# Expert-choice layers of a two-layer diffusion block: weight chunks in runs of 8 KB, token gathers spread over the experts, layer norms in pairs

## The chip, the cores and the metric

One core of one Trainium2 chip runs the whole program in one launch. The metric is device time in microseconds (us), the median of three runs. A lower time is better.

## The reference, cut to what matters

The block has two layers on 256 latent tokens and 256 context tokens of width 1024, all in float32. Each layer mixes tokens by four branches, projects, normalises, and then runs an expert-choice feed-forward part: each of 16 experts picks its 32 best tokens of a stream (latent or context), and its output goes back to those tokens, weighted by the gate.

```python
x = layer_norm(alpha * x + g1 * y, ln1_g, ln1_b)
h = x * (1 + sc2) + sh2
aff = softmax(h @ w_router)                     # 256 tokens x 16 experts
gval, idx = top_k(aff.T, 32)                    # 32 tokens of each expert
xg = h[idx]
y = (silu(xg @ w_gate) * (xg @ w_up)) @ w_down  # three 1024 x 1024 matrices per expert
f = zeros.at[idx].add(y * gval)
x = layer_norm(alpha * x + g2 * f, ln2_g, ln2_b)
```

In layer 0 this is done for both streams (context and latent have their own modulation but share the experts); in layer 1 for the latent stream alone. The expert weights are 2 x 16 x 3 matrices of 4 MB.

## The kernel before

Tokens lie on the 128 partitions, so a tile of tokens is 128 x 1024: tiles 0 and 1 are the context, 2 and 3 the latent stream. `xz` holds the tiles of the residual stream (four in layer 0, two in layer 1). The program text is a dataflow; a scheduler orders each engine's instructions when the program is built, by program order as priority and by readiness, so instructions of neighbouring steps are interleaved, and each engine then runs its list in order.

`out_project` (L1167) writes the last mixer result into `xz`. With the last column group (g = 3) it takes for each tile the statistics (`ln_stats`, L1207: two `bn_stats`, one `bn_aggr`, and `rsqrt`, L109, a chain of 11 small VectorE operations on 128 x 1), then for the tile before it the router logits (`route`, L1276: eight transposes, two copies, eight matmuls, two VectorE operations) and the normalisation in place (`ln_hat`, L1220). The last tile's normalisation stands in `moe` at L1369.

`moe` (L1297) issues the loads of expert 0's weights first, then softmax and top-k on VectorE (L1357 to L1391), then the experts. Weights come in chunks of 256 rows, 1 MB each: 12 chunks an expert, 192 a layer, all issued by SP in the order in which they are used (`wl`, L1326). A chunk's 256 rows are laid as `(k p) f -> p k f`: row p and row 128 + p on partition p, so each partition gets two runs of 4 KB. Slots are taken in turn from a list: buffers of 2048 floats per partition take a whole chunk in one DMA (tile `w`, or `we` where the tile has another name); pairs of 1024 floats take the two halves in two DMAs of 512 KB (`we`). Layer 0 has 13 slots in turn, 7 of them whole; layer 1 has 18, of which 11 are whole. A few chunks of expert 0 go to tiles that are free only then (`early`, L1320): in layer 0 three of the four `xg` tiles. A chunk's slot is free when its last matmul has read it; SP waits for that before it issues the next DMA in line, and everything behind it on SP waits as well.

`gather(g)` (L1398) builds the inputs of four experts, transposed, as `xgT`: one-hot matrices OH by VectorE (one operation per token tile and stream), then matmuls of 128 x 128 of `xz` with OH, each of them two PE records since float32 takes two passes: 64 records a group in layer 0, 32 in layer 1, with an ACT or DVE evacuation each. Group 0 is interleaved with expert 0's matmuls; group 1 comes in expert 1 after gate and up, group 2 in expert 2 after gate and up, group 3 at the end of expert 2, followed by `residual` (L1430), which overwrites `xz` by `alpha * (xz * g + b)` with 32 PE records and 8 to 16 VectorE operations. After every fourth expert the outputs `ys` are scattered into `xz` (L1505 to L1537). The last scatter is added in PSUM (`fin_tiles`, L1539), and `ln_last` (L1227) normalises one tile after the other: in layer 0 one half of a tile by ACT and one by DVE, and layer 1 begins with `make_h` (L267), which transposes the tiles; in layer 1 it writes the output.

Of the kernel before, what the change touches and what calls it, by code (L numbers as in the profile page):

```python
# [91 lines left out]
class Net:  # L92
# [1074 lines left out]
    def out_project(self, l):  # L1167
# [39 lines left out]
    def ln_stats(self, t, src=None):  # L1207

        nc = self.nc
        z = self.xt(t)  # L1210
        st = self.sm.tile([P, 2, 6], F32, tag="bst", name="bst")
        for j in range(2):
            nc.vector.bn_stats(st[:, j], src[j] if src else z[:, j * 512:(j + 1) * 512])
        mv = self.sm.tile([P, 2], F32, tag="bmv", name="bmv")
        nc.vector.bn_aggr(mv, st)
        rs = self.sm.tile([P, 1], F32, tag="brs", name="brs")
        self.rsqrt(rs, mv[:, 1:2], 1, "l")
        return mv[:, 0:1], rs

    def ln_hat(self, t, stats=None):  # L1220

        nc = self.nc
# [4 lines left out]
    def ln_last(self, l, t, src, rows):  # L1227

        nc = self.nc
        z = self.xt(t)  # L1230
        mu, rs = self.ln_stats(t, src)
        if l == 0:
            nb = self.sm.tile([P, 1], F32, tag="lnb", name="lnb")
            nc.vector.tensor_scalar(nb, mu, rs, -1.0, op0=OP.mult, op1=OP.mult)
            nc.scalar.activation(z[:, 0:512], src[0], AF.Identity, scale=rs, bias=nb)
            nc.vector.tensor_scalar(z[:, 512:1024], src[1], mu, rs, op0=OP.subtract, op1=OP.mult)
# [519 lines left out]
```

## Time and profile before

| what | value |
|---|---|
| median of three runs | 2164.75 us (2156.14 to 2170.97) |
| the profiled execution's own time | 2166.49 us |
| its span, first to last instruction | 2164.7 us |
| PE busy | 1849.5 us (85%) |
| DVE, ACT, POOL busy | 946.1, 503.9, 341.2 us |
| DMA moved | 553.92 MB, mean 256 GB/s |
| DMA share of queue q1 | 66.2% of 16 engines' span |

The whole program is one core's; busy times are sums over stages with different limits, so they are read by stage. The share of the DMA engines and GB/s over 40 slices of 54 us show two stretches at about 409 GB/s: the experts of layer 0 (about 720 to 1205 us) and of layer 1 (about 1695 to 2146 us). PE runs at a granted clock of 2.4 GHz where the row says 1.00 and at 1.2 GHz where it says 0.50.

### The profile page before, as it was taken

Reading aid. Unit: us, or ns where it says so; the run is one execution under the profiler, and the core shown is the slowest. Engines: PE = TensorE matmul, PEld = TensorE weight load, DVE = VectorE, ACT = ScalarE, POOL = GpSimd, SP = SyncE. Lnnn points to the kernel's source line nnn. Section 1 sums busy time; section 2 is a strip of 40 time slices with the busy share of each in tenths; the row PEclk is TensorE's granted clock in tenths of the full one; section 3 lists DMA queues with packets and bytes.
Section 4 is the critical chain, followed back from the end, with each engine's and each line's share of the span. In section 5 each row is a group of like instructions: output and inputs, shape, how many; then the busy total and the mean of one; then the engine's idle time right before and its main releaser. Section 6 shows DMA issues by size and latency. Waiting matters only on the chain. (4 is left out here: it accounts for less than half of the span.)

```text
span 2164.7 us, 33549 instructions
## 1 busy us (share of the span) xinstructions
PE 1849.5 (85%) x13730; PEld 1198.9 (55%) x13730; DVE 946.1 (44%) x2139; ACT 503.9 (23%) x1037; POOL 341.2 (16%) x366
## 2 busy tenths in 40 slices
PE   6899899988999899988887898898989886676665
PEld 2677778877879454322222576788889542222221
DVE  3859457854226324121121586967655330010102
ACT  2332217742221110000000332346443110000000
POOL 1151320014431000000000134321274000000000
PEclk9999999999999899999999998989999897776867
DMA  7546412137333599999999465303487899999996
GB/s 291 175 157 209 147 65 88 40 115 251 112 136 112 220 385 347 410 409 409 409 409 409 161 227 183 98 23 106 151 271 268 325 408 409 409 409 409 409 409 255
DMA packets 200182, 553.92 MB, mean 256 GB/s; under 512 B 16223, under 2 KB 83165, under 8 KB 194397
## 3 DMA queue, kind: packets, MB, share of 16 engines
q1 hardware_dynamic: 190960, 538.56, 66.2%
q10 hardware_dynamic: 9068, 13.23, 1.7%
q8 instruction: 108, 1.77, 0.3%
q14 instruction: 46, 0.37, 0.1%
HBM read 541.25 MB, written 10.49 MB: 255 GB/s over the span
## 5 line engine op out<-in xcount | busy, mean ns | idle before, releaser
L1461 PE MATMUL ps_gu<-w,xgT 128*32 128x256 f32 (+1 forms) x1632 | 241.5, 534 | 68.3 <-DMA w<-in_w_up_e_dram 35.0
L149 POOL TENSOR_TENSOR wl<-w,wh 128x1024 fp32r<-128x1024 f32 x62 | 155.2, 2503 | 894.6 <-ACT wh L148 805.4
L1461 PE MATMUL ps_gu<-we,xgT 128*32 128x256 f32 (+1 forms) x1440 | 204.0, 509 | 44.2 <-DMA we<-in_w_up_e_dram 26.3
L1461 PEld LDWEIGHTS ps_gu<-w,xgT 128*32 128x32 f32 (+1 forms) x1632 | 78.3, 134 | 210.5 <-issue 81.1
L1503 DVE TENSOR_TENSOR y<-ps_dn,g2r 32x512 f32<-32x512 f32 (+1 forms) x128 | 70.9, 554 | 254.3 <-PE ps_dn L1492 252.8
L311 PE MATMUL ps_gate<-hh,wh 128*128 128x512 f32 (+1 forms) x512 | 179.4, 351 | 0.4 <-ACT wh L148 0.4
L313 PE MATMUL ps_gate<-hh,wl 128*128 128x512 f32 (+1 forms) x512 | 179.7, 351 | 0.0
L312 PE MATMUL ps_gate<-hl,wh 128*128 128x512 f32 (+1 forms) x512 | 178.2, 348 | 0.0
L148 ACT CAST wh<-w 128x1024 fp32r<-128x1024 f32 x124 | 129.3, 1048 | 178.1 <-PE ps_gate L312 78.2
L1461 PEld LDWEIGHTS ps_gu<-we,xgT 128*32 128x32 f32 (+1 forms) x1440 | 62.0, 127 | 171.9 <-DMA we<-in_w_up_e_dram 63.7
L1492 PE MATMUL ps_dn<-w,eaT 128*32 128x256 f32 (+1 forms) x896 | 119.3, 524 | 28.8 <-DMA w<-in_w_down_e_dram 21.9
L1471 ACT ACTIVATE eth<-ps_gu 128x512 f32<-128x512 f32 (+1 forms) x32 | 15.7, 491 | 515.8 <-PE ps_gu L1461 515.8
L312 PE MATMUL ps_n<-wl,hh 128*128 128x256 f32 x400 | 116.6, 291 | 6.7 <-POOL wl L149 6.7
L1474 DVE SCALAR_TENSOR_TENSOR eac<-eth,ps_gu 128x512 f32<-128x512 f32 (+1 forms) x32 | 17.7, 555 | 238.9 <-PE ps_gu L1461 238.9
L311 PE MATMUL ps_n<-wh,hh 128*128 128x256 f32 x400 | 117.4, 294 | 5.5 <-DVE c_qk L872 3.6
L149 DVE TENSOR_TENSOR wl<-w,wh 128x1024 fp32r<-128x1024 f32 x62 | 85.8, 1384 | 72.4 <-ACT wh L148 72.1
L313 PE MATMUL ps_n<-wh,hl 128*128 128x256 f32 x400 | 116.7, 292 | 0.0
L1492 PE MATMUL ps_dn<-we,eaT 128*32 128x256 f32 (+1 forms) x640 | 91.2, 492 | 17.6 <-DMA we<-in_w_down_e_dram 13.2
L311 PEld LDWEIGHTS ps_gate<-hh,wh 128*128 128x128 f32 x512 | 98.9, 193 | 11.2 <-ACT wh L148 0.8
L313 PEld LDWEIGHTS ps_gate<-hh,wl 128*128 128x128 f32 x512 | 99.1, 193 | 10.8 <-DVE wl L149 0.2
L312 PEld LDWEIGHTS ps_gate<-hl,wh 128*128 128x128 f32 x512 | 98.7, 193 | 10.8
L1473 DVE SCALAR_TENSOR_TENSOR eth<-eth,ps_gu 128x512 f32<-128x512 f32 (+1 forms) x32 | 17.8, 555 | 193.6 <-ACT eth L1471 193.6
(452 smaller groups left out, 3579.4 us busy)
## 6 DMA issues: line engine op xcount, KB each, us to landing
w<-in_w_gate_e_dram SPq DMA_DIRECT2D x75, 1024.0 KB, 13.2
w<-in_w_down_e_dram SPq DMA_DIRECT2D x72, 1024.0 KB, 12.7
w<-in_w_up_e_dram SPq DMA_DIRECT2D x62, 1024.0 KB, 13.3
we<-in_w_up_e_dram SPq DMA_DIRECT2D x120, 512.0 KB, 13.6
w<-in_w_in_dram SPq DMA_DIRECT2D x54, 1024.0 KB, 5.6
we<-in_w_down_e_dram SPq DMA_DIRECT2D x108, 512.0 KB, 14.0
we<-in_w_gate_e_dram SPq DMA_DIRECT2D x96, 512.0 KB, 13.6
w<-in_w_mod_dram SPq DMA_DIRECT2D x44, 1024.0 KB, 5.1
```

The costliest lines, as they stand in the source:

```text
L148: nc.scalar.copy(h, w)
L149: (nc.gpsimd if j else nc.vector).tensor_tensor(x, w, h.bitcast(F32), op=OP.subtract)
L311: nc.tensor.matmul(ps, lh[k], rh[k], start=(k == 0), stop=False)
L312: nc.tensor.matmul(ps, lh[k], rl[k], start=False, stop=False)
L313: nc.tensor.matmul(ps, ll[k], rh[k], start=False, stop=(k == nk - 1))
L1461: nc.tensor.matmul(ps[M * q:M * q + M, :NF], xg[e // 4][:, 2 * kk + k, e % 4, :], w[k][:, q * NF:(q + 1) * NF], start=(kk == 0 and k == 0) ...
L1471: nc.scalar.activation(th, pss[0][:, :NF], AF.Tanh, scale=0.5)
L1473: nc.vector.scalar_tensor_tensor(th, th, 1.0, pss[0][:, :NF], op0=OP.add, op1=OP.mult)
L1474: nc.vector.scalar_tensor_tensor(ac, th, 0.5, pss[1][:, :NF], op0=OP.mult, op1=OP.mult)
L1492: nc.tensor.matmul(py[M * q:M * q + M, :NF], av[:, fc % nj, fc // nj, :], w[k][:, q * NF:(q + 1) * NF], start=(fc == 0), stop=(fc == 7))
L1503: nc.vector.tensor_tensor(ys[w][32 * e4:32 * e4 + 32, q * NF:(q + 1) * NF], py[o:o + 32, :NF], g2r[o:o + 32, q * NF:(q + 1) * NF], op=OP.mult)
```

## The change

1. Expert weights: a chunk's rows are laid as `(p k) f`, so that partition p gets rows 2p and 2p + 1, which lie next to each other in memory. A whole chunk becomes one run of 8 KB a partition; halves stay runs of 4 KB, now every second row. What the weights multiply is laid to match: features are taken in pairs (`pairs`), so the transposes of `xz`, of the activations and the gather's stationary operand read every second float. The modulation columns are brought into that order by `in_pairs` (16 small matmuls in layer 0, 8 in layer 1, two copies), the router's weights by their DMA.
2. `residual` writes to own tiles `acc` and `xz` stays, so that gathers can come later: group 1 in expert 2, group 2 in expert 6, group 3 in expert 10. `residual` moves to the end of expert 1. `xg` has two buffers in place of four; `acc` takes their room, and takes part of the early chunks.
3. Norms: two tiles share one `rsqrt` chain. In `out_project` the statistics are taken for pairs; the last two tiles are normalised by ACT in `moe`. `ln_last` runs for two tiles; in layer 0 ACT does three of four halves.
4. The one-hot operations of a group become one operation.

```diff
@@ merge
+        oh = self.mg.tile([P, 2, 512], F32R, tag="oh", name="oh", bufs=1)
         nc.sync.dma_start(oT[:, :, :n], self.oT[br])
         ol = self.mg.tile([P, 2, 512], F32R, tag="ol", name="ol", bufs=1)
-        oh = self.mg.tile([P, 2, 512], F32R, tag="oh", name="oh", bufs=1)
@@ out_project
                 if g == 3:
-                    stats[t] = self.ln_stats(t)
                     if t > t0:
-                        self.route(t - 1, stats[t - 1])
-                        self.ln_hat(t - 1, stats[t - 1])
-        self.route(3, stats[3])
-        self.last_stats = stats[3]
+                        pl[t - 1] = self.route(t - 1)
+                    if t % 2:
+                        mu, rs = self.ln_pair([self.halves(t - 1), self.halves(t)])
+                    elif t > t0:
+                        for i in range(2):
+                            self.logits(i, pl[i], mu[:, i:i + 1], rs[:, i:i + 1])
+                        for i in range(2):
+                            self.ln_hat(i, mu[:, i:i + 1], rs[:, i:i + 1])
+        pl[3] = self.route(3)
+        for i in range(2):
+            self.logits(2 + i, pl[2 + i], mu[:, i:i + 1], rs[:, i:i + 1])
+        self.last_stats = mu, rs
+    def pairs(x):
+        return x.rearrange("p (a q j) -> p a j q", q=P, j=2)
+    def ln_pair(self, srcs):
+        mv = self.sm.tile([P, 2, 2], F32, tag="bmv", name="bmv")
+        for i, src in enumerate(srcs):
...
+                nc.vector.bn_stats(st[:, j], src[j])
+            nc.vector.bn_aggr(mv[:, i], st)
+        self.rsqrt(rs, mv[:, :, 1], 2, "l")
+    def ln_hats(self, t, mu, rs):
+        nc.vector.scalar_tensor_tensor(nb, mu, -1.0, rs, op0=OP.mult, op1=OP.mult)
+        for i in range(2):
+            z = self.xt(t + i)
+            nc.scalar.activation(z, z, AF.Identity, scale=rs[:, i:i + 1], bias=nb[:, i:i + 1])
@@ ln_last (layer 0)
+                    if i and j:
+                        nc.vector.tensor_scalar(o, src[i][j], mu[:, i:i + 1], r, op0=OP.subtract, op1=OP.mult)
+                    else:
+                        nc.scalar.activation(o, src[i][j], AF.Identity, scale=r, bias=nb[:, i:i + 1])
+    def in_pairs(self, name, cols):
...
+        for i, c in enumerate(cols):
+            cv = c.rearrange("p (a h) -> p h a", h=2)
+            for h in range(2):
+                for j in range(2):
+                    nc.tensor.matmul(pv[64 * h:64 * h + 64, j, i], self.c("ident").rearrange("p (m j) -> p j m", j=2)[:, j],
+                                     cv[:, h], start=True, stop=True)
...
@@ route
-                nc.tensor.transpose(ps[j][:, k * P:(k + 1) * P], z[:, kc * P:(kc + 1) * P], self.c("ident"))
+                nc.tensor.transpose(ps[j][:, k * P:(k + 1) * P], self.pairs(z)[:, kc // 2, kc % 2], self.c("ident"))
@@ moe
-                early = {x: [(px, "xg", 4)] for x in (7, 8, 9)}
+                early = {7: [(px, "xg", 2)], 8: [(px, "acc", 2)], 9: [(px, "acc", 2)]}
                 early[10] = [(mg, "ol", 1), (pe, "y1", 1)]
             else:
-                early = {7: [(px, "xg", 4)] * 2, 8: [(px, "xg", 4), (mg, "ol", 1)]}
+                early = {7: [(px, "acc", 1)], 8: [(px, "xg", 2), (mg, "ol", 1)]}
...
-                rows = src[l, e, kk * 256:(kk + 1) * 256, :].rearrange("(k p) f -> p k f", p=P)
+                rows = src[l, e, kk * 256:(kk + 1) * 256, :].rearrange("(p k) f -> p k f", k=2)
+                flat = src[l, e, kk * 256:(kk + 1) * 256, :].rearrange("(p k) f -> p (k f)", k=2)
...
-                    w = self.wload(rows, (2, 1024), pool=slot)
+                    w = self.wload(flat.unsqueeze(1), (1, 2048), pool=slot)
...
-            self.ln_hat(3, self.last_stats)
+            self.ln_hats(2, *self.last_stats)
...
-                for i in range(2):
-                    for wi in range(nw):
-                        onehot(g, i, wi, OH[:, i, wi])
+                onehot(g, OH)
...
-                                nc.tensor.matmul(po, self.xz[:, off[w] + i, k * P:(k + 1) * P],
+                                nc.tensor.matmul(po, self.pairs(self.xz[:, off[w] + i])[:, k // 2, k % 2],
                                                  OH[:, i, wi].rearrange("p e c -> p (e c)"), start=(i == 0), stop=(i == 1))
...
-                        z = self.xz[:, t, j * 512:(j + 1) * 512]
-                        nc.vector.tensor_tensor(z, z, gb[0], op=OP.mult)
+                        cs = slice(j * 512, (j + 1) * 512)
+                        z = acc[t // 2][:, t % 2, cs]
+                        nc.vector.tensor_tensor(z, self.xz[:, t, cs], gb[0], op=OP.mult)
                         nc.vector.tensor_tensor(z, z, gb[1], op=OP.add)
...
-                if e in (1, 2):
-                    self.all_of(gather(e))
-                if e == 9 and l == 1:
-                    rows = list(self.norm_rows(1, lambda nm: px.tile([P, 1024], F32, tag="xg", name=nm, bufs=4)))
+                if e in (2, 6, 10):
+                    self.all_of(gather(e // 4 + 1))
+                if e == 11 and l == 1:
+                    free = [self.xz[:, t] for t in range(2)]
+                    rows = list(self.norm_rows(1, lambda nm: free.pop(0)))
...
-                    nc.tensor.transpose(ps[:, j * P:(j + 1) * P], ac[:, j * P:(j + 1) * P], self.c("ident"))
+                    nc.tensor.transpose(ps[:, j * P:(j + 1) * P], self.pairs(ac)[:, j // 2, j % 2], self.c("ident"))
...
-                if e == 2:
-                    self.all_of(gather(3))
+                if e == 1:
+                    acc = [px.tile([P, 2, 1024], F32, tag="acc", name="acc", bufs=nw) for _ in ws]
                     residual()
```

## Rows read from the trace of the kernel before

**Rows 1.** The page, the span in 40 equal slices: what the DMA engines moved.
```profile
GB/s 291 175 157 209 147 65 88 40 115 251 112 136 112 220 385 347 410 409 409 409 409 409 161 227 183 98 23 106 151 271 268 325 408 409 409 409 409 409 409 255
```

**Rows 2.** Windows of both expert stages: busy us (records) per engine, PEclk, DMA share, GB/s.
```profile
core 0: us, PE busy (x) PEld busy (x) DVE busy (x) ACT busy (x) POOL busy (x), PEclk, DMA share, GB/s
720.00:760.00 40.00, 40.00 (x225) 18.80 (x225) 7.38 (x16) 4.87 (x10) 0.00 (x0) 1.00 0.60 220
760.00:840.00 80.00, 80.00 (x453) 45.45 (x451) 28.84 (x58) 13.88 (x29) 0.00 (x0) 1.00 0.90 352
840.00:1200.00 360.00, 310.18 (x1300) 94.15 (x1298) 71.70 (x122) 16.95 (x30) 0.00 (x0) 1.00 1.03 408
1690.00:1700.00 10.00, 9.36 (x71) 7.06 (x72) 3.58 (x14) 1.96 (x4) 0.00 (x0) 0.78 0.22 70
1710.00:2140.00 430.00, 302.78 (x3108) 121.31 (x3100) 59.05 (x136) 20.35 (x50) 0.00 (x0) 0.77 1.03 408
```

**Rows 3.** The chain that ended last, from the first long DMA of layer 1's experts.
```profile
1746.99 0.27 PE ps_gb L1440 x3
1747.26 18.64 DMA w<-in_w_down_e_dram
```

**Rows 4.** DMA issues of whole chunks: count, KB each, median us to landing.
```profile
w<-in_w_gate_e_dram SPq DMA_DIRECT2D x75, 1024.0 KB, 13.2
w<-in_w_down_e_dram SPq DMA_DIRECT2D x72, 1024.0 KB, 12.7
w<-in_w_up_e_dram SPq DMA_DIRECT2D x62, 1024.0 KB, 13.3
```

**Rows 5.** Windows at the program's start, while modulation weights load.
```profile
10.00:22.00 12.00, 9.02 (x34) 1.83 (x34) 1.77 (x11) 0.28 (x2) 0.00 (x0) 1.00 1.03 416
14.00:16.00 2.00, 2.00 (x12) 0.39 (x8) 0.00 (x0) 0.00 (x0) 0.00 (x0) 1.00 1.02 408
18.00:20.00 2.00, 1.50 (x10) 0.27 (x6) 0.00 (x0) 0.00 (x0) 0.00 (x0) 1.00 1.05 424
```

**Rows 6.** SP's timeline there: whole chunks (L127), halves (L231).
```profile
11.10 3.61 SPq L231 DMA_DIRECT2D wm<-in_w_mod_dram  x2
17.90 0.33 SPq L127 DMA_DIRECT2D w<-in_w_mod_dram  x1
```

**Rows 7.** PE's timeline in layer 0, experts 0 to 3.
```profile
747.28 5.47 PE L1492 MATMUL ps_dn<-we,eaT 128*64 128x512 f32 x24
...
768.02 5.64 PE L1416 MATMUL ps_xg<-OH,xz 128*128 128x128 f32 x44
...
799.82 5.64 PE L1416 MATMUL ps_xg<-OH,xz 128*128 128x128 f32 x44
...
825.30 2.84 PE L1440 MATMUL ps_gb<-const,lgb 128*128 128x128 f32 x24
```

**Rows 8.** DVE's timeline in layer 1, from the last logits to the softmax.
```profile
1680.24 0.23 DVE L1294 SCALAR_TENSOR_TENSOR rlg<-wrb,bmv,ps_lg 128x16 f32<-128x16 f32 x1 [1.54 <-PE ps_lg L1292]
1680.39 0.15 DVE L121 SCALAR_TENSOR_TENSOR rs_y<-rs_t,rs_y 128x1 f32<-128x1 f32 x1
1682.62 0.18 DVE L1357 TENSOR_REDUCE rmx<-rlg 128x2 f32<-128x32 f32 x1
```

**Rows 9.** The seam of the layers: PE's transposes of the new tiles.
```profile
1220.35 1.54 PE L280 MATMUL ps_h<-const,xz 128*128 128x128 f32 x6 [2.08 <-ACT xz L1235]
1225.67 1.12 PE L280 MATMUL ps_h<-const,xz 128*128 128x128 f32 x4 [1.33 <-DVE hf L285]
```

**Rows 10.** DVE's timeline at the end of layer 1.
```profile
2150.11 0.70 DVE L1213 BATCH_NORM_STATS2 bst<-ps_fin 128x6 f32<-128x512 f32 x1 [1.33 <-PE ps_fin L1530]
...
2160.37 1.42 DVE L1241 SCALAR_TENSOR_TENSOR xz<-xz,brs,l2b_r 128x512 f32<-128x512 f32 x2
```

**Rows 11.** PE's short matmuls before the experts.
```profile
1649.90 1.97 PE L1268 MATMUL ps_wrb<-wrs,ones 128*128 128x32 f32 x16
...
691.97 0.90 PEld L1287 LDWEIGHTS ps_xT<-const,xz 128*128 128x128 f32 x8
```

More of the change, by code (lines that the diff above doesn't have):

```diff
@@ L1205, in which, with halves @@
         return 0 if t >= 2 else 1
-    def ln_stats(self, t, src=None):
+    def halves(self, t):
+        return [self.xt(t)[:, j * 512:(j + 1) * 512] for j in range(2)]
+    def ln_pair(self, srcs):
+        nc = self.nc
+        mv = self.sm.tile([P, 2, 2], F32, tag="bmv", name="bmv")
+        for i, src in enumerate(srcs):
+            st = self.sm.tile([P, 2, 6], F32, tag="bst", name="bst")
+            for j in range(2):
+                nc.vector.bn_stats(st[:, j], src[j])
+            nc.vector.bn_aggr(mv[:, i], st)
+        rs = self.sm.tile([P, 2], F32, tag="brs", name="brs")
+        self.rsqrt(rs, mv[:, :, 1], 2, "l")
+        return mv[:, :, 0], rs
@@ L1209, in ln_stats, with ln_hat @@
+    def ln_hat(self, t, mu, rs):
         nc = self.nc
         z = self.xt(t)
[L1211 to L1218, printed above, removed]
@@ L1229, in ln_last @@
+    def ln_last(self, l, t, src, rows, z):
         nc = self.nc
-        z = self.xt(t)
-        mu, rs = self.ln_stats(t, src)
+        mu, rs = self.ln_pair(src)
         if l == 0:
[L1233 to L1236, printed above, removed]
-            return
@@ L1238, in ln_last @@
-        for j in range(2):
-            cs = slice(j * 512, j * 512 + 512)
-            nc.vector.scalar_tensor_tensor(z[:, cs], src[j], mu, rows[0][:, cs], op0=OP.subtract, op1=OP.mult)
-            nc.vector.scalar_tensor_tensor(z[:, cs], z[:, cs], rs, rows[1][:, cs], op0=OP.mult, op1=OP.add)
-            (nc.sync, nc.scalar)[j].dma_start(self.a["out"][0, (t - 2) * P:(t - 1) * P, cs], z[:, cs])
+            nb = self.sm.tile([P, 2], F32, tag="lnb", name="lnb")
+            nc.vector.scalar_tensor_tensor(nb, mu, -1.0, rs, op0=OP.mult, op1=OP.mult)
@@ L1252, in comb @@
         return cg, cb
+    def in_pairs(self, name, cols):
+        nc = self.nc
+        n = len(cols)
+        ps = self.pt.tile([P, 512], F32, tag="t", name="ps_pair")
+        pv = ps[:, :8 * n].rearrange("p (j i a) -> p j i a", j=2, i=n)
+        for i, c in enumerate(cols):
+            cv = c.rearrange("p (a h) -> p h a", h=2)
+            for h in range(2):
+                for j in range(2):
+                    nc.tensor.matmul(pv[64 * h:64 * h + 64, j, i], self.c("ident").rearrange("p (m j) -> p j m", j=2)[:, j],
+                                     cv[:, h], start=True, stop=True)
+        out = self.keep.tile([P, 4, 8], F32, tag="c2p", name=name, bufs=1)[:, :n]
+        for j in range(2):
+            nc.vector.tensor_copy(out.rearrange("p i (a j) -> p i a j", j=2)[:, :, :, j], pv[:, j])
+        return out
     def router_weights(self, l):
@@ L1292, in route, with logits @@
             nc.tensor.matmul(pl[:, 0:16], self.xT[:, i, k, :], self.wrs[w][:, k, 0:16], start=(k == 0), stop=(k == 7))
-        lg = self.lg[:, i]
+        return pl
+    def logits(self, t, pl, mu, rs):
+        nc = self.nc
+        w = self.which(t)
+        lg = self.lg[:, t - self.qtiles[0]]
         nc.vector.scalar_tensor_tensor(lg, self.wrb[w][:, 0:16], mu, pl[:, 0:16], op0=OP.mult, op1=OP.add)
@@ L1448, in moe @@
             g0 = next(first)
-            ys = rows = None
+            ys = rows = acc = None
             for e in range(NE):
@@ L1482, in moe @@
                 if e == NE - 1:
[L1484 removed]
+                    fin = {off[0] + i: self.fin_tiles(acc[off[0] // 2][:, i], pool, tag) for i, (pool, tag) in
                            enumerate(((self.pg, "g"), (self.pm, "m")))}
@@ L1543, in fin_tiles @@
             r.append(pool.tile([P, 512], F32, tag=tag, name="ps_fin"))
-            self.nc.tensor.matmul(r[hf], self.c("ident"), self.xz[:, i, hf * 512:hf * 512 + 512], start=True, stop=False)
+            self.nc.tensor.matmul(r[hf], self.c("ident"), z[:, hf * 512:hf * 512 + 512], start=True, stop=False)
         return r
```

77 lines of the change are left out of this document (44 added, 33 removed).

## The prediction

> **What bounds the kernel now.** I read the slices of the page first, to find the stages: two long stretches at about 409 GB/s, which are the experts of the two layers, each with a dip ahead of it [rows 1]. Windows over these stretches tell what stands still. From 840 to 1200 us and from 1710 to 2140 us the DMA engines are busy all the time at 408 GB/s, and PE is not: 310 of 360 us and 303 of 430 us [rows 2]. The chain of waits says the same of layer 1: from 1747 us on it holds DMA after DMA [rows 3]. So for some 800 us the weight stream is the bound. A chunk of 1.0486 MB takes 2.57 us at 408 GB/s, and 12 chunks, an expert, 30.8 us.
>
> Ahead of these stretches the DMA stands still for want of free slots, because PE is late. In layer 0 PE is busy for 40 of 40 us and for 80 of 80 us while the DMA moves 220 and 352 GB/s [rows 2]: idle DMA of 40 x (1 - 220/408) = 18.4 us and 80 x (1 - 352/408) = 11.0 us. In layer 1 there is one hole, 70 GB/s for 10 us, so 8.3 us, and then none: PE works off three gathers until 1747 us, but 18 slots of look-ahead keep the DMA full. A microsecond of PE or VectorE counts there only before that hole ends; in layer 0 it counts until about 840 us.
>
> **The change part by part.** Sums are against the profiled execution, 2166.5 us (span 2164.7 us and 1.8 us around it); the median of the runs lies 1.7 us below.
>
> *Runs of 8 KB.* How many chunks: 7 of 13 slots are whole in layer 0 and 11 of 18 in layer 1; the whole chunks before are mostly the 75 + 72 + 62 of the DMA issues [rows 4]. Halves keep 4 KB. How fast: the program's start has both kinds. There the modulation weights load in whole chunks with one run of 8 KB a partition and in halves with runs of 4 KB that lie 24 KB apart. While the halves issued at 11.10 us were on their way the rate was 408 GB/s, as in the experts, and just after a whole chunk was issued at 17.90 us it was 424; over 12 us of both kinds it was 416, about halfway [rows 5, 6]. So I take 424 for 8 KB and no change for 4 KB runs that are apart. A whole chunk then takes 2.47 us, 0.097 less. In the stretches that the DMA bounds there are 360/2.57 = 140 chunks and 430/2.57 = 167, of which 7/13 and 11/18 are whole: 75 + 102 = 177. The gain is 177 x 0.097 = 17.2 us. Bounds: with 416, 177 x 0.049 = 9 us; above 424, since that window still holds some halves, up to an estimated 24 us. Nothing is late behind it: PE has 50 us to spare in 360 in layer 0 and 127 in 430 in layer 1 [rows 2].
> The Trainium skill (DMA: Bandwidth & Descriptors, section "Why small descriptors are slow (HBM only)") speaks against so much: a packet costs about 3 cycles beside its beats of 32 bytes, so 128 + 3 and 256 + 3 cycles, and the gain would be 1.1%, an estimated 5 us in place of 17.2. The rows have 3.9% between 408 and 424; they are short windows, so the rule stays as a rival.
>
> *Gathers spread.* A gather of layer 0 is 64 records; 44 take 5.64 us [rows 7], so 64 take 8.2 us. Two of three leave the time before 840 us, and so 16.4 us of PE. Is that more than the DMA stood still there? 24 records of the down matmuls take 5.47 us [rows 7], three chunks, so 1.8 us a chunk. Experts 1 and 2 then need 24 x 1.8 + one gather 8.2 + `residual` 32 x 0.118 = 3.8 [rows 7] = 55 us and some 2 us for two turns through the activation; the stream needs 24 x 2.57 = 61.7 us. PE is no longer the slower one, and of the 11.0 us of idle DMA I count 9.5 as gone (bounds 0 and 11). The gathers now in experts 6 and 10 cost 8.2 us of PE where it has 50/360 x 30.8 = 4.3 us to spare an expert; 13 slots, 33 us of stream, cover that until PE has caught up after one or two experts. If this cover were gone, some 4 us would be paid each time, 8 in all. In layer 1 the same move gains nothing, since the DMA never stood still after the hole, and costs nothing.
>
> *The chain before the experts.* In layer 1 the last logits arrive at 1680.24 us; then come the rest of the last tile's root, one more logits step and the normalisation, and the softmax begins at 1682.62 [rows 8]. With one root for two tiles, begun when the statistics are there, it is done before the logits arrive; two or four steps of 0.2 us stay, and the normalisation goes to ACT, which has nothing to do during top-k. That is 1.7 us, in front of the hole; layer 0 has the same lines, so 3.4 in both (bounds 1.5 and 4.5: ACT's exponential may wait behind a normalisation). The shared one-hot operation makes the first gather wait for one longer operation, at most about 0.5 us a layer, as the 0.70 us of a 512-wide operation [rows 10] against the short ones; I count 0.
>
> *The last norms.* At the seam PE waits for the tiles: transposes at 1220.35 for the second tile and at 1225.67 for the last [rows 9]. Two chains of 11 steps go, and two halves go from DVE to ACT; but a pair waits for its second tile. I take 2.5 us (0 to 3.5). At the end DVE works from 2150.11 to 2161.79 [rows 10]; one chain goes, 11 steps of 0.15 us [rows 8] and the gaps between them, some 2 us, but it ran partly between long operations, and now the first tile waits for the second: 1 us (from 0.5 lost to 2).
>
> *What is added.* `in_pairs` is 16 and 8 small matmuls, 32 and 16 records; the nearest row has 16 records in 1.97 us [rows 11], so 3.9 + 2.0 us, on PE ahead of the experts where PE is the bound. They depend on nothing late and can fill a wait of PE, so 0 to 5.9; I take 3. The stationary operand of transposes and gathers is now read with every second float. No row shows such a read. The nearest is the packed one, 8 loads in 0.90 us [rows 11]. Below, a read cannot gain; above, if each took twice as long, a record would start every 0.24 us in place of 0.12. I take 0, since the row's loads run beside the matmuls.
> On this the Trainium skill (SBUF — State Buffer, section "Door 1: The DMA port swizzle", its note on cachelines) says that lines are of 16 bytes and two hits a line keep full speed; a step of two floats has two. No run here shows it.
>
> Sum: 17.2 + 9.5 + 3.4 + 3.5 - 3 = 30.6 us off, from 2166.5 to 2135.9, and 1.7 lower for the median, 2134.2: I say 2135. With the low bounds (9 + 4 + 1.5 + 0 - 6) some 8 to 10 us are left, 2155; with the high ones 2120.
>
> **The rivals.** (a) *Long runs give little.* The 424 is an edge of a 2 us window and the engines move 4 and 8 KB alike. For it: the 416 contains transfers that began earlier. Against it: 416 holds over 12 us, with halves at 408 in the middle. Then 13 to 17 us are left of 31: about 2150.
> (b) *The gathers' gain comes back.* The late gathers meet a PE with 4.3 us to spare and stop the stream, or `residual`, now in expert 1, holds PE up as much as gather 1 did. Then 9.5 us go: about 2144. Against it: PE needs 57 us where the stream needs 62.
> (c) *Reads of every second float are slow; the kernel gets slower.* Place: the transposes of `route` (64 and 32 records), gather 0 (64 and 32) and half of gather 1 (32), 224 records in stretches that PE bounds. At x us more a record the price is 224x; with 0.14 the 31 us are used up. Twice the cadence (0.12) gives 2162, no change; if a load could no longer run beside the matmul before it, some 0.25 more each, 56 us, gives about 2190.
>
> **How the numbers follow.** The forecast has 0.68, (a) 0.14, (b) 0.11, (c) 0.07. The forecast's own spread, from the bounds, is 2120 to 2150. For 8 in 10 I reach from 2118 to 2154, which takes in (a) and (b) and leaves (c) out. A measurement of this kernel can tell about 1% from no change, 21.6 us, so below 2143 counts as faster: nine tenths of the forecast and half of (b), together 0.69. Within 1% are (a), the rest of (b) and of the forecast and a part of (c), 0.26; slower by over 1% is most of (c), 0.05.
>
> **What would show it.** Right: the long windows at some 416 to 418 GB/s in place of 408 (7/13 of the bytes at 424); in layer 0 no dip after about 755 us, expert 3 beginning some 18 us earlier; ps_xg records in three later places with the DMA at full rate there; softmax less than 1 us after the last logits. Wrong: 408 again in the long windows (a); a dip in experts 6 or 10 of layer 0, or still one at 800 us (b); ps_xT and ps_xg records further than 0.13 us apart (c). The forecast as a whole falls if the stream is no faster and the dip stays.

## The result, and the profile after

| | before | after |
|---|---|---|
| median of the runs | 2163.58 us (4 runs) | 2139.02 us (4 runs, 2131.03 to 2151.01) |
| profiled execution | 2166.49 us | 2131.03 us |
| its span | 2164.7 us | 2129.1 us |

The ratio after to before is 0.9869, 95% interval 0.9837 to 0.9901: 28 us less, 21 to 35 (the two medians lie 24.6 us apart). Two more series of the same kernel gave 0.9868 (0.9828 to 0.9907) and 0.9856 (0.9818 to 0.9894). The forecast was 2135, its range 2118 to 2154.

The profiled execution of after is the fastest of its series, so the two traces differ by more (35.6 us) than the kernels do. I therefore cut the traces into stages between marks on PE, and the three executions of the same kernel after show how much of a stage is chance. The marks are tiles: ps_xT are the transposes of `route` and ps_lg the logits, ps_af and ps_pos the first and last transposes of top-k, ps_xg a gather, ps_gu the gate and up products of an expert, ps_aT the transposes of its activation, ps_fin the last scatter, ps_h the transposes at the seam. *L0 start*: from the end of the last logits to the first transpose (ps_aT) of expert 4. *L0 rest*: from there to that of expert 15. *Seam*: to the last ps_h group. *Mixer*: to the end of the last logits of layer 1. *L1*: to the ps_aT of expert 15. *End*: to the end of the last ps_fin.

| kernel, us | L0 start | L0 rest | seam | mixer | L1 | end |
|---|---|---|---|---|---|---|
| before | 170.0 | 320.7 | 36.1 | 449.9 | 457.2 | 16.1 |
| after | 161.3 | 313.0 | 34.3 | 444.2 | 448.6 | 17.5 |
| after, second | 160.9 | 313.5 | 34.0 | 456.5 | 448.7 | 14.8 |
| after, third | 161.3 | 313.1 | 34.3 | 453.6 | 449.6 | 17.1 |

The stages of the experts repeat within 1 us, so they can be read one by one: 8.8 + 7.5 + 1.9 + 8.2 = 26.4 us less with the means of after. The end, 14.0 to 17.5 us in all kernels of this document, is left out. The mixer holds little of the change (the small matmuls of in_pairs and the end of out_project) and takes 444 to 457 us with one and the same kernel; in the pair of traces it gave 5.7 us of the 35.6, and the stretch ahead of the first mark, 703.5 us before and 699.3, 707.5 and 703.1 after, gave 4.2.

The slices and the packets of the page of after, to be held against [rows 1], and the packets of before:

```profile
GB/s 296 169 168 203 159 66 80 50 81 263 122 121 118 229 366 415 416 416 415 415 416 416 177 221 189 97 19 105 182 267 253 328 416 416 417 417 415 416 416 255
DMA packets 170596, 553.91 MB, mean 260 GB/s; under 512 B 15182, under 2 KB 82124, under 8 KB 136268
...
DMA packets 200182, 553.92 MB, mean 256 GB/s; under 512 B 16223, under 2 KB 83165, under 8 KB 194397
```

The same bytes now go in 29586 packets fewer. The long stretches stand at 416, and the first of them is full from its second slice. The windows over the same stages, to be held against [rows 2]:

```profile
core 0: us, PE busy (x) PEld busy (x) DVE busy (x) ACT busy (x) POOL busy (x), PEclk, DMA share, GB/s
720.00:760.00 40.00, 40.00 (x217) 19.40 (x218) 7.45 (x13) 4.32 (x8) 0.00 (x0) 1.00 0.69 249
760.00:840.00 80.00, 78.90 (x379) 35.48 (x375) 30.61 (x51) 7.10 (x14) 0.00 (x0) 1.00 1.02 416
840.00:1170.00 330.00, 302.50 (x1328) 105.80 (x1326) 67.76 (x106) 21.71 (x41) 0.00 (x0) 1.00 1.02 416
1710.00:2100.00 390.00, 271.10 (x2661) 103.98 (x2659) 47.57 (x106) 17.28 (x42) 0.00 (x0) 0.76 1.02 416
...
900.00:920.00 20.00, 18.52 (x90) 8.28 (x88) 2.79 (x6) 2.32 (x5) 0.00 (x0) 1.00 1.02 417
960.00:980.00 20.00, 18.99 (x96) 8.73 (x94) 3.01 (x6) 3.01 (x6) 0.00 (x0) 1.00 1.02 414
1015.00:1035.00 20.00, 19.62 (x96) 8.68 (x96) 2.79 (x6) 2.32 (x5) 0.00 (x0) 1.00 1.02 417
```

The dip to 352 between 760 and 840 is gone. The last three windows lie where PE works on the late gathers (the scheduler took half of gather 2 as early as expert 4, at 847.5 to 860.5 us, and half of gather 3 in expert 8): PE is busy for 92 to 98% of them, and the DMA moves 414 to 417 GB/s all the same. The 220 of 720 to 760 has become 249 and no more.

The chain in front of the experts, DVE's timeline in layer 1, to be held against [rows 8] (a gap in front of an instruction stands in brackets, with what ended it):

```profile
1652.17 0.23 DVE L1346 SCALAR_TENSOR_TENSOR rlg<-wrb,bmv,ps_lg 128x16 f32<-128x16 f32 x1 [0.69 <-PE ps_lg L1338]
1652.32 0.15 DVE L119 TENSOR_TENSOR rs_t<-rs_v,rs_y 128x2 f32<-128x2 f32 x1
...
1652.70 0.16 DVE L121 SCALAR_TENSOR_TENSOR brs<-rs_t,rs_y 128x2 f32<-128x2 f32 x1
1652.90 0.38 DVE L1347 SCALAR_TENSOR_TENSOR rlg<-rlg,brs,wrb 128x16 f32<-128x16 f32 x2
...
1653.31 0.19 DVE L1410 TENSOR_REDUCE rmx<-rlg 128x2 f32<-128x32 f32 x1
1653.53 0.19 DVE L1412 TENSOR_TENSOR rex<-rlg,rmx 128x32 f32<-128x32 f32 x1
1654.78 0.19 DVE L1415 TENSOR_REDUCE rsm<-rex 128x2 f32<-128x32 f32 x1 [1.05 <-ACT rex L1413]
```

ACT's timeline there:

```profile
1653.38 1.24 ACT L1248 ACTIVATE xz<-xz,lnb,brs 128x1024 f32<-128x1024 f32 x1 [2.37 <-DVE lnb L1245]
1654.53 0.21 ACT L1413 ACTIVATE rex<-rex 128x32 f32<-128x32 f32 x1
```

The softmax begins 1.14 us after the last logits in place of 2.38 us. But it stops 1.05 us for its exponential (0.30 before), since ACT took the normalisation of 1.24 us first. And the root was not done before: DVE runs its list in order, and the last three steps of the root (1652.32 to 1652.86) stand in it behind the logits step at 1652.17 that waited for PE.

PE at the seam, to be held against [rows 9]:

```profile
1199.43 0.47 PE L280 MATMUL ps_h<-const,xz 128*128 128x128 f32 x1 [4.45 <-ACT xz L1263]
1200.10 3.52 PE L280 MATMUL ps_h<-const,xz 128*128 128x128 f32 x15 [0.20 <-ACT xz L1263]
...
1207.87 0.60 PE L280 MATMUL ps_h<-const,xz 128*128 128x128 f32 x4
```

One wait of 4.45 us for ACT stands here, then the transposes run nearly through; the stage is 1.9 us shorter.

### The profile page after: what moved, and what is told of

Read it like the earlier page. It is cut to its first block, busy times and chain, and to the rows that moved or that the text cites. A ratio compares the mean times of both kernels' runs of the same rounds, so it can differ in the third digit from the quotient of the medians.

```text
span 2129.1 us, 33529 instructions
## 1 busy us (share of the span) xinstructions
PE 1846.2 (87%) x13778; PEld 1204.2 (57%) x13778; DVE 936.1 (44%) x2023; ACT 509.6 (24%) x1043; POOL 340.3 (16%) x366
## 5 line engine op out<-in xcount | busy, mean ns | idle before, releaser
L1517 PE MATMUL ps_gu<-w,xgT 128*32 128x256 f32 (+1 forms) x1632 | 236.3, 519 | 52.2 <-DMA w<-in_w_gate_e_dram 29.5
L311 PE MATMUL ps_n<-wh,hh 128*128 128x256 f32 x400 | 117.1, 293 | 6.4 <-DVE c_qk L872 3.6
L313 PE MATMUL ps_n<-wh,hl 128*128 128x256 f32 x400 | 116.3, 291 | 0.0
L311 PEld LDWEIGHTS ps_gate<-hh,wh 128*128 128x128 f32 x512 | 98.1, 192 | 11.1 <-ACT wh L148 0.8
L313 PEld LDWEIGHTS ps_gate<-hh,wl 128*128 128x128 f32 x512 | 97.9, 191 | 10.6 <-DVE wl L149 0.2
L1532 DVE SCALAR_TENSOR_TENSOR eac<-eth,ps_gu 128x512 f32<-128x512 f32 (+1 forms) x32 | 17.7, 554 | 189.1 <-PE ps_gu L1517 189.0
L1531 DVE SCALAR_TENSOR_TENSOR eth<-eth,ps_gu 128x512 f32<-128x512 f32 (+1 forms) x32 | 17.7, 554 | 181.8 <-ACT eth L1529 181.8
## 6 DMA issues: line engine op xcount, KB each, us to landing
w<-in_w_down_e_dram SPq DMA_DIRECT2D x72, 1024.0 KB, 12.6
```

What stands on the lines that cost most here:

```text
L311: nc.tensor.matmul(ps, lh[k], rh[k], start=(k == 0), stop=False)
L313: nc.tensor.matmul(ps, ll[k], rh[k], start=False, stop=(k == nk - 1))
L1517: nc.tensor.matmul(ps[M * q:M * q + M, :NF], xg[e // 4][:, 2 * kk + k, e % 4, :], w[k][:, q * NF:(q + 1) * NF], start=(kk == 0 and k == 0) ...
L1531: nc.vector.scalar_tensor_tensor(th, th, 1.0, pss[0][:, :NF], op0=OP.add, op1=OP.mult)
L1532: nc.vector.scalar_tensor_tensor(ac, th, 0.5, pss[1][:, :NF], op0=OP.mult, op1=OP.mult)
```

## The experiments

All kernels ran with the kernel before beside them, so ratios are to it. The stages of each, measured as above:

| kernel, us | L0 start | L0 rest | seam | mixer | L1 | end | ratio |
|---|---|---|---|---|---|---|---|
| e_runs_only | 171.0 | 315.8 | 36.0 | 453.5 | 449.5 | 14.0 | 0.9918 (0.9892 to 0.9945) |
| e_no_runs | 160.0 | 319.7 | 33.9 | 452.0 | 456.8 | 14.3 | 0.9933 (0.9906 to 0.9959) |
| e_2kb | 161.1 | 332.7 | 34.0 | 451.4 | 472.0 | 16.0 | one time, 2191.12 us |
| e_old_gathers | 172.4 | 316.0 | 34.1 | 443.7 | 449.1 | 15.2 | 0.9884 (0.9838 to 0.9930) |
| e_double_gather | 162.1 | 319.1 | 34.0 | 461.6 | 450.0 | 16.5 | one time, 2168.34 us |
| e_unit_step | 161.1 | 313.7 | 33.8 | 442.9 | 449.0 | 16.7 | 0.9828 (0.9774 to 0.9881) |
| e_g2r_early | 158.4 | 314.0 | 33.9 | 445.6 | 448.0 | 15.5 | 0.9878 (0.9831 to 0.9925) |
| e_best | 157.6 | 314.1 | 34.0 | 458.9 | 448.3 | 14.8 | 0.9895 (0.9865 to 0.9925) |
| e_warm | 156.5 | 314.1 | 34.0 | 451.3 | 449.9 | 16.8 | 0.9860 (0.9817 to 0.9903) |
| e_warm_two | 156.5 | 314.0 | 34.0 | 449.6 | 447.2 | 16.6 | 0.9864 (0.9825 to 0.9902) |

The L0 start of the same traces, cut once more at the marks ps_pos, first ps_gu and ps_aT:

| kernel, us | last logits to ps_pos | to the first ps_gu | to ps_aT of expert 0 | to ps_aT of expert 4 |
|---|---|---|---|---|
| before | 10.9 | 5.9 | 25.7 | 127.5 |
| e_runs_only | 10.9 | 6.9 | 25.7 | 127.5 |
| e_no_runs | 10.1 | 5.7 | 27.1 | 117.1 |
| e_unit_step | 10.1 | 6.7 | 27.1 | 117.1 |
| after, all three | 10.1 | 5.6 to 6.0 | 27.4 | 117.7 |
| e_old_gathers | 10.1 | 6.0 | 27.4 | 128.8 |
| e_g2r_early | 10.1 | 6.3 | 25.7 | 116.3 |
| e_best | 9.5 | 6.2 | 25.7 | 116.3 |
| e_warm, e_warm_two | 9.5 | 5.1 | 25.7 | 116.3 |

In the three executions of after three of the four parts repeat to 0.01 us. The part from ps_pos to the first ps_gu does not; it is the one with the low clock (below).

**The runs alone, and all but the runs**

```diff
-rows = src[l, e, kk * 256:(kk + 1) * 256, :].rearrange("(k p) f -> p k f", p=P)
+rows = src[l, e, kk * 256:(kk + 1) * 256, :].rearrange("(p k) f -> p k f", k=2)
+flat = src[l, e, kk * 256:(kk + 1) * 256, :].rearrange("(p k) f -> p (k f)", k=2)
```

> The kernel before, with one edit: a whole expert chunk is read with rows 2p and 2p+1 in partition p, so one run of 8 KB in place of two of 4 KB; halves likewise read row 2p or 2p+1. The columns of the tokens are not paired to match, so the product is another one; the number and size of all instructions is that of the kernel before. Theory (run length is worth 0.097 us a whole chunk, 177 chunks in the stretches that the DMA bounds): about 17 us less than before, long windows 840:1200 and 1710:2100 at some 416 GB/s, the dip in 760:840 unchanged or deeper. Rival (a packet costs 3 cycles beside its beats, 1.1%): about 5 us less, windows at 411. Rival (run length does nothing, the rate of after came from PE keeping the slots free): 0, windows at 408.

> The kernel after without its first part: chunks in two runs of 4 KB a partition, no pairing, no small matmuls; gathers, residual and norms as after. Theory: the 17 us of the run length come back and the 3 us of the pairing go, so some 14 us above after, windows at 408 GB/s, no dip after 760 us. Rival (3 cycles a packet): 2 us above after, windows at 412. Rival (the rate came with the spread gathers): as after, windows at 416.

Windows of e_runs_only (the columns as above):

```profile
762.00:842.00 80.00, 80.00 (x451) 44.68 (x446) 28.65 (x58) 13.28 (x28) 0.00 (x0) 1.00 0.90 350
900.00:1180.00 280.00, 239.86 (x1008) 71.38 (x1005) 54.75 (x91) 12.21 (x21) 0.00 (x0) 1.00 1.02 416
1800.00:2110.00 310.00, 201.44 (x2036) 70.60 (x2036) 34.20 (x80) 10.54 (x26) 0.00 (x0) 0.78 1.02 416
```

Windows of e_no_runs:

```profile
770.00:850.00 80.00, 78.90 (x385) 35.50 (x381) 30.12 (x50) 7.68 (x15) 0.00 (x0) 1.00 1.02 409
900.00:1180.00 280.00, 249.94 (x1090) 84.08 (x1088) 58.32 (x90) 17.19 (x33) 0.00 (x0) 1.00 1.03 409
1800.00:2120.00 320.00, 214.58 (x2104) 81.20 (x2104) 36.57 (x82) 13.29 (x32) 0.00 (x0) 0.75 1.03 409
```

The rate follows the runs and not the gathers: 416 with them under the old gathers, 409 without them under the new ones. Both rivals, 411 and 412 or an unchanged rate, are out. In the two stages that the DMA bounds, the runs are worth 4.9 + 7.7 = 12.6 us against before, and 6.5 + 7.8 = 14.3 between e_no_runs and after. In the L0 start they give and cost nothing: e_runs_only is 1.0 us longer there than before, but all of it lies between ps_pos and the first ps_gu, and from there on the two kernels are equal, as e_no_runs and e_unit_step are. The whole time of e_runs_only is 17.7 us below before, but with an interval of 12 to 23.

**Runs of 2 KB**

```diff
-flat = ....rearrange("(p k) f -> p (k f)", k=2)
+flat = ....rearrange("(k p) (h f) -> p h k f", p=P, h=2)
```

> The kernel after with whole chunks read in four runs of 2 KB a partition (rows p and 128+p, each in two column halves laid side by side); halves stay at 4 KB; the columns then don't match, so the product is another one. Theory (408 GB/s with 256 packets and 424 with 128 for each sixteen-engine chunk: a fixed time for each packet, 0.00076 us of a chunk's 2.57): whole chunks at 379, so the long windows at 392 GB/s in layer 0 (7 of 13 slots whole) and 390 in layer 1. Rival (3 cycles beside 64 beats): whole chunks at 399, windows at 403. Rival (8 KB is special, below it length does not matter): 408.

Windows of e_2kb:

```profile
900.00:1180.00 280.00, 244.61 (x1050) 83.22 (x1046) 55.60 (x86) 16.93 (x32) 0.00 (x0) 0.99 1.04 397
1800.00:2160.00 360.00, 243.97 (x2292) 91.92 (x2288) 37.83 (x85) 14.35 (x35) 0.00 (x0) 0.71 1.04 395
```

397 and 395 lie between my 392 and 390 and the rival's 403. Taken apart with halves at 408.5, the rate of whole chunks comes out of 1/397 = (6/13)/408.5 + (7/13)/r: r is 388, and 387 from layer 1 (7/18 and 11/18). The same sum turns the 416 of after into 423 and 421. So a chunk takes 2.71 us at 2 KB, 2.57 at 4 KB and 2.48 at 8 KB. The 256 packets more cost 0.14 us, the 128 fewer save 0.08: some 0.0006 us a packet both times, and 16 engines share the chunk, so 9 to 10 ns of an engine for each. That is the law that I expected, with a constant smaller by a fifth.

The single packets in the traces say the same: in the long windows of before, after and e_2kb one of 2 KB takes 88.6 ns on the mean, one of 4 KB 163 to 164 in every kernel, close together or every second row, and one of 8 KB 314. So 12 to 14 ns of each do not grow with its length; by the rates it is less, which fits a DMA share above 1 (1.02 to 1.04): an engine's packets overlap a little.

The Trainium skill (DMA: Bandwidth & Descriptors, "Why small descriptors are slow (HBM only)") gives by its 3 cycles a packet an estimated 1.1% from 4 to 8 KB and 2.3% from 4 to 2 KB. The runs show 3.3% and 5.5%, and the measurement decides.

**The old gathers**

```diff
-if e in (2, 6, 10):
-    self.all_of(gather(e // 4 + 1))
+if e in (1, 2):
+    self.all_of(gather(e))
...
+if e == 2:
+    self.all_of(gather(3))
+    residual()
```

> The kernel after without its second part: gathers 1 to 3 and residual in experts 1 and 2 again, in place on the tokens, four gather tiles, three early chunks in them; runs of 8 KB, pairing and norms as after. Theory: the DMA stands still again between 760 and 840 us, 350 to 365 GB/s there, expert 3 of layer 0 begins 9.5 us later and the kernel takes 9 to 12 us more than after (a faster stream would wait longer). Rival (the late gathers of after stop the stream as much as they saved): within 2 us of after, and after's windows of experts 6 and 10 lower than this kernel's. Layer 1: no difference in either.

The window of e_old_gathers that answers to 760 to 840 of after:

```profile
765.00:845.00 80.00, 79.90 (x447) 45.82 (x444) 28.04 (x55) 13.34 (x28) 0.00 (x0) 1.00 0.89 347
```

As expected: the dip is back, 347 GB/s with PE busy throughout. The price is 11.2 us in the L0 start (11.1 of it behind expert 0) and 2.8 in the rest, 14.0, above the 9 to 12 that I gave; the intervals of the whole times are too wide to show it. A DMA that could move 416 stands still for 80 x (1 - 347/416) = 13.3 us here, and for 11.0 at 408: a faster stream loses more to the same dip. Layer 1 is the same in both, 449.1 and 449.0.

**How much a late gather may cost**

```diff
-for i in range(2):
+for i in [0, 1] * (2 if g >= 2 else 1):
     nc.tensor.matmul(po, ..., start=(i == 0), stop=(i == 1))
```

> The kernel after with every matmul of gathers 2 and 3 issued twice (the second pair starts the sum anew, so the result is the same): the suspected price of a late gather, 8.2 us of PE in layer 0, is 16.4. Theory (13 slots are 33 us of stream, and PE has some 4 us to spare in each expert, so 17 us in the four experts up to the next gather): nothing is lost, 313 to 315 us from the activation of expert 4 to that of expert 15 in layer 0 (after: 313), windows at 416 throughout. Rival (a late gather stops the stream, the more so the longer it is): 8 us more for each of the two, 325 to 330 us, with a slice below 400 behind expert 6 or 10. In layer 1 nothing in either.

Windows of e_double_gather:

```profile
1130.00:1140.00 10.00, 8.48 (x40) 2.91 (x38) 0.69 (x1) 0.59 (x1) 0.00 (x0) 1.00 0.72 272
1140.00:1150.00 10.00, 9.01 (x40) 2.23 (x36) 2.75 (x4) 0.00 (x0) 0.00 (x0) 1.00 0.94 332
```

319.1 us, 6 more than after: my number (313 to 315) was wrong, and the rival's 325 to 330 as well. From 850 to 1130 us, while the doubled gathers ran (860 to 1056), one window of 10 us fell to 376 GB/s (890 to 900, 1.0 us lost); all others stood at 409 or more. Most of the loss stands in one place, 1130 to 1150: 10 x (1 - 272/416) + 10 x (1 - 332/416) = 5.5 us. SP's timeline there:

```profile
1127.87 0.33 SPq L127 DMA_DIRECT2D w<-in_w_gate_e_dram  x1
1136.36 4.90 SPq L1399 DMA_DIRECT2D we<-in_w_gate_e_dram  x6
```

For 8 us SP issues nothing. These are the first chunks of expert 14, and experts 14 and 15 by the code use the first list of slots alone, 7 in place of 13. So I read it thus: PE's lag, which 13 slots had covered, was paid when the look-ahead shrank, and in after PE has caught up by then (411 to 419 GB/s from 1120 to 1160). The sum of late PE work would then have a limit between one and two gathers each, set where the slots get few. No run changed the list, so the cause is read from the place and the code, in one execution.

**Reads of every second float, and the pairing**

```diff
-return x.rearrange("p (a q j) -> p a j q", q=P, j=2)
+return x.rearrange("p (a j q) -> p a j q", q=P, j=2)
...
-self.c2p = self.in_pairs(...)
```

> The kernel after, with runs of 8 KB, but every operand read with a step of one float again and without the 48 small matmuls of the pairing; the columns then don't match the rows, so the product is another one. Theory: the pairing costs what its small matmuls take and next to nothing for the step of two, so 3 us less than after (0 to 6), windows at 416 as after. Rival (reads of every second float are slow where PE is the bound): over 10 us less than after. Rival (the small matmuls fill a wait of PE): within 1 us of after.

The loads and matmuls of ps_xT in after (min/median/max in ns, first and last start, form):

```profile
L1334 PEld LDWEIGHTS ps_xT<-const,xz x48: 197/209/262, 681.8 to 1650.0; 128*128 128x128 f32 x48
L1334 PE MATMUL ps_xT<-const,xz x48: 281/283/344, 681.9 to 1650.1; 128*128 128x128 f32 x48
```

The same in e_unit_step:

```profile
L1333 PEld LDWEIGHTS ps_xT<-const,xz x48: 139/141/225, 683.4 to 1650.3; 128*128 128x128 f32 x48
L1333 PE MATMUL ps_xT<-const,xz x48: 272/273/308, 683.5 to 1650.4; 128*128 128x128 f32 x48
```

PE's timeline of after at the two places of in_pairs:

```profile
485.84 1.17 PE L1293 MATMUL ps_pair<-c,const 128*64 128x4 f32 x32
...
1617.60 0.67 PE L1293 MATMUL ps_pair<-c,const 128*64 128x4 f32 x16
```

The step of two does cost: a load of 141 ns takes 209, and a matmul 10 ns more. The load runs beside the matmul before it, so most of that is hidden: two transposes start 120 ns apart in place of 109, two records of a gather 118 in place of 112. On the path this is 0.9 us in the L0 start, 0.3 in expert 0 (27.4 against 27.1) and 0.6 up to expert 4 (117.7 against 117.1). The whole L0 start hides it, 161.1 against 161.2, since e_unit_step happened to take 6.7 us from ps_pos to the first ps_gu.

The small matmuls take 1.10 and 0.60 us before the next one starts, 1.7 in all. The ratio of e_unit_step is the lowest of all, but beside these 0.9 us it differs from after only in the mixer (442.9), which is chance (below).

The Trainium skill (SBUF — State Buffer, "Door 1: The DMA port swizzle") says that two hits to a 16-byte line keep full speed. The load of ps_xT, half as long again, does not agree; that of ps_xg, which goes from 192 to 196 ns, nearly does.

**Taking more of PE's work away from the start**

```diff
-if e == 0:
-    self.rowbcast(g2r, [self.mcol(l, 5, w) for w in ws])
...
 nc.vector.tensor_copy(W, ps[:R, :256])
+g2r = pe.tile([P, 1024], F32, name="g2r", bufs=1)
+self.rowbcast(g2r, [self.mcol(l, 5, w) for w in ws])
```

> The kernel after with the spreading of the second gate (64 and 8 matmuls of rowbcast into g2r) issued at the start of top-k, where PE waits 6 us, in place of behind expert 0's gate and up. Theory: PE bounds the start of the experts, so its 3.2 us in layer 0 and 1 us in layer 1 leave the path, and gather 0 finds a PE that has worked just before, with a higher granted clock than the 0.56 of after: 4 to 7 us less than after; in layer 0 first ps_gu 2 us sooner behind ps_pos. Rival (the DMA's free slots and not PE bound this stretch): within 1 us of after.

```diff
-self.ln_hats(2, *self.last_stats)
...
+self.ln_hats(2, *self.last_stats, sm[:, 0:2])
...
-if i and hf:
+if l == 1 and hf:
+    self.ln_last(l, t + self.xt0, [fin[t]], rows, [acc[0][:, t]])
+elif i and hf:
```

> The version above with two more edits: ACT's normalisation of the last pair waits for the softmax, so that the exponential goes first, and the last norm of layer 1 goes tile by tile as before. Theory: 0.8 us in each layer ahead of top-k and 1 us at the end, so 2 to 3 us below e_g2r_early and 6 to 10 below after. Rival (ACT's order and the pairing of the tail cost nothing): equal to e_g2r_early; last logits to ps_af 3.5 us as in after, and 17 us from the activation of expert 15 to the last ps_fin.

```diff
-self.rowbcast(g2r, [self.mcol(l, 5, w) for w in ws])
+for _ in range(2 if l == 0 else 4):
+    self.rowbcast(g2r, [self.mcol(l, 5, w) for w in ws])
```

> The kernel of e_best with the spreading of the second gate issued twice (layer 0) and four times (layer 1) during top-k, the same values written again, so that PE works through nearly all of top-k. Theory (the 1.2 GHz of the first gather comes from PE's idle 6 us before it): the granted clock of the 5 us behind ps_pos is above 0.9 in place of 0.56 in after and 0.72 in e_best, the first ps_gu comes 4.3 to 4.8 us behind ps_pos in place of 6.0 and 6.2, and expert 4's activation 155 to 156 us behind the last logits (after 161, e_g2r_early 158.4, e_best 157.6). Rival (the clock there has another cause, or the first gather waits for its one-hot rows and evictions): 6 us and 157.6 us as in e_best. The total: 2 us less than e_best, which no interval here can show, since the mixer of layer 1 alone took 444 to 459 us with the same code.

> The kernel of e_warm with two issues of the spreading in layer 1 as well, in place of four: there 64 records took 9.60 us and ran 3.3 us past the end of top-k. Theory: layer 0 as in e_warm (156.5 us from the last logits to the activation of expert 4), layer 1 from the last logits to ps_pos 9.2 us as in e_best (e_warm: 12.5) and to the activation of expert 15 some 447 us (after 448.6, e_best 448.3, e_warm 449.9), so 5 to 6 us less than after in the stages of the experts. Rival (in layer 1 the DMA bounds at once, so nothing of this counts): 448.6. The total: below after by about as much, which the interval may not show.

PE of after in the 5 us behind ps_pos:

```profile
709.40:714.40 5.00, 4.98 (x35) 4.47 (x36) 2.94 (x6) 0.91 (x2) 0.00 (x0) 0.50 0.27 111
```

The same of e_warm:

```profile
709.70:714.70 5.00, 3.96 (x30) 3.66 (x30) 3.63 (x7) 2.04 (x5) 0.00 (x0) 1.00 0.41 170
```

Step by step the L0 start falls from 161.2 to 158.4 (the spreading out of the way), 157.6 (the exponential first: last logits to ps_af 2.9 us in place of 3.6) and 156.5 (PE at work during top-k). For e_g2r_early I had given 4 to 7 us; it is 2.8 here and 1.0 in L1, less 0.8 in the L0 rest, and the first ps_gu came no sooner behind ps_pos (6.3 us): PE waits 1.04 us there for the one-hot rows, does 28 gather records ahead of it in place of 22, and the granted clock stays at 0.66.

The last pair of rows shows the clock: after an idle 6 us PE works at 0.50 to 0.63 in the three executions of after, 0.50 being 1.2 GHz, and after a top-k filled with matmuls at 1.00, 2.4 GHz; the first ps_gu comes 5.1 us behind ps_pos in place of 6.2 in e_best. My 4.3 to 4.8 was missed, since DVE's one-hot rows make PE wait 1.04 us here too.

In layer 1 the four issues of e_warm overran top-k (12.5 us from the last logits to ps_pos); with two it is 9.3, and L1 447.2 in place of 449.0, in one execution.

My 2 to 3 us for e_best below e_g2r_early were wrong: the exponential gives 0.8 us in layer 0 and nothing in L1 (448.3 against 448.0), and the unpaired tail gives nothing: from the last ps_fin to the end it takes 11.2 us, as before the change, and the paired one 10.6 to 10.9 in after.

So e_warm_two is 5.7 us below after in the two stages of the experts (470.5 + 447.2 against 474.4 + 449.0 us, from the last logits to expert 15). In the whole time nothing of it is to be seen: 2141.34 against 2139.29 us beside each other.

> The kernel after, unchanged, on the same chip as e_warm_two, so that the two are compared beside each other. Theory: 161 us and 448.6 us in the two stages as before; in the total 4 to 6 us above e_warm_two. Rival: no difference.

**The kernel after once more**

> The kernel after, unchanged, beside the two versions below on one chip. Theory (the stretches that the change does not touch differ from run to run by the length of stretches at 1.2 GHz): the mixer of layer 1, from the last ps_h of layer 0 to the last logits of layer 1, takes anything from 443 to 453 us, whichever kernel it is; the stages that the change touches repeat within 2 us (161 us from the last logits to the activation of expert 4 in layer 0, 449 us from the last logits to the activation of expert 15 in layer 1). Rival (the change shortens the mixer by its order of instructions): 444 us again.

The mixer took 456.5 us here, above the 453 that I gave, and 453.6 in the third series, the experts' stages what they had taken, so the order of instructions is not what made it 444. One window of 50 us in it, begun 170 us after the last ps_h, tells where the time goes. Of e_g2r_early (mixer 445.6), then after (444.2), then e_double_gather (461.6):

```profile
1379.00:1429.00 50.00, 47.85 (x744) 41.84 (x742) 35.85 (x101) 23.54 (x62) 15.52 (x20) 1.00 0.08 26
```

```profile
1377.90:1427.90 50.00, 47.89 (x719) 41.17 (x717) 35.53 (x101) 22.75 (x61) 15.15 (x20) 0.93 0.08 25
```

```profile
1397.40:1447.40 50.00, 48.42 (x577) 41.58 (x575) 27.45 (x74) 18.59 (x47) 12.80 (x16) 0.69 0.07 23
```

The code is the same, PE is busy for the same 48 us, and the records done are 744, 719 and 577: the granted clock is 1.00, 0.93 and 0.69. In e_double_gather three windows of 10 us in a row stand at 0.50.

## Why the prediction was right, step by step

**The bound.** Right: with 416 in place of 408 the stretches in which PE had time to spare became shorter in proportion, and layer 1 did not notice where its gathers stood.

**Runs of 8 KB.** The mechanism was right, the term too large: 17.2 was forecast, 12.6 to 14.3 measured. The step that failed is the 424, the edge of a window of 2 us in [rows 5]: whole chunks move at 421 to 423, so 0.08 us a chunk in place of 0.097, and 177 x 0.08 is 14. In the L0 start, where PE bounds, the runs gave nothing; the sum had counted next to none of it. Rival (a), about 2150 us, did not come: the rate stands in all long windows of kernels with these runs, and e_2kb shows the law from the other side, in one execution.

**Gathers.** 9.5 was forecast with 11.0 as the bound. It was 11.4 with runs of 4 KB (before against e_no_runs: 10.4 from expert 0 to expert 4 and 1.0 in the rest) and 13.9 with 8 KB (after against e_old_gathers: 11.1 and 2.8). The upper bound was wrong, since I worked it out with the old rate; the two parts help each other. My 57 us of PE for two experts, a gather and `residual` were right: in after it is 57.2 us from ps_aT of expert 1 to that of expert 3. Rival (b) fell: the stream does not stop at the late gathers. The 33 us of cover were as I said for one gather, and not for two.

**The chain.** 3.4 was forecast, 0.7 (last logits to ps_af in layer 0, 4.3 to 3.6) and 0.5 (to ps_pos in layer 1, 10.44 to 9.97) were measured, below my lower bound. The root does not end before the logits arrive, and the bound that I named, the exponential behind a normalisation, is what happened.

Gather 0 starts 0.4 us later behind ps_pos, but not for want of its one-hot rows: the scheduler put 18 of the spreading's small matmuls in front of it in place of 10 (1.49 us in place of 1.06), and e_g2r_early, with the same shared one-hot operation, starts it 1.32 us behind ps_pos, as before (1.31). Expert 0 then needs 27.4 us from its first ps_gu to its activation, 25.7 before. 0.3 of this is the step of two; the rest is the order on PE, as two neighbouring rows of after show:

```profile
722.36 1.07 PE L1517 MATMUL ps_gu<-w,xgT 128*64 128x512 f32 x2
...
724.03 1.08 PE L1517 MATMUL ps_gu<-w,xgT 128*64 128x512 f32 x4
```

Two records take as long as four: where the products with both column halves of the weights stand together, their records run beside each other (at 723.73 us in before two of them start 7 ns apart). Up to the activation after has 12 such groups between its gather matmuls and before 11, which is 1.0 us, and 42 gather records where before has 38, 0.7 us; 8 matmuls of the spreading less take 0.2 off. The scheduler's order thus cost 1.4 us, about as much as the shorter chains gave in both layers (1.2).

**Seam and tail.** 2.5 and 1 were forecast, 1.9 and 0.3 to 0.5 measured.

**What is added.** 3 was forecast for in_pairs, 1.7 measured. The 0 for the step of two was 0.9 us in the L0 start. Rival (c) fell: the price of the step of two is 6 to 11 ns a record where I had needed 140 to lose the gain. (I had counted 96 records for the transposes of `route`; the trace has 48, which changes nothing at that price.)

Together: by stages 26.4 + 0.3 - 1.7 = 25 us off, 30.6 forecast; the whole times say 28 (21 to 35). Too much for the runs and the chain was partly made up by too little for the gathers, and that was luck. Of the 35.6 us between the two traces, 5.7 in the mixer and 4.2 ahead of the first mark are not the change's, which only further executions of the same kernel could tell. One slip stays: the low end of the forecast, 2155, took 4 us for the gathers where the bound named for them was 0; with 0 it is about 2160.

## What to carry to other kernels

Where a stream bounds, count packets and not only bytes: 4 to 8 KB gave 3.3% on the chunks that changed and 1.8% on the stream here, and the gain is to be had only where nothing else holds the stream up, so take PE's work out of its way first. Work that is late enough may be put under a full look-ahead for nothing, up to the place where the look-ahead gets shorter. And judge small edits by stages between marks in the trace, cut so fine that the part which varies stands alone; else chance in one part hides a price in another, as it did with the step of two. The whole time of this kernel moves by 10 us or more for other reasons.

## What was not expected of the hardware

The spread of the run times has two places. One is the stretch ahead of the first mark, 699 to 716 us, in which the granted clock stands at 0.50 for 31 to 65 us in all. The other is the mixer of layer 1, with 24 to 65 us of it; the three executions of after have 27, 48 and 58 us there, and the mixer takes 444, 454 and 457. One stretch varies most: PE's granted clock falls to 0.50 for none to 30 us, from one execution to the next, with nearly the same code and the same busy time; the mixer takes 443 to 462 us over all kernels. The stretch follows one of small matmuls (ps_z and ps_y, 32 by 32: 131 records in 3 us of before's mixer) and then 3 us with 10 records, in which PE waits. What sets its length was not tried. Behind top-k, on the other hand, the low clock came in layer 0 in each execution of the kernels that do not fill top-k with matmuls (0.50 to 0.66 over the 5 us behind ps_pos), and filling PE's idle time took it away.
